# Dense tokens' rows kept in DRAM for most of the kernel, and gate blocks read back eight at a time instead of four

## The chip, the cores and the metric

The kernel runs on one core of a Trainium2 chip. The metric is the device time of one execution in microseconds (us), the median of several runs. The engines named below are PE (TensorE matmul), PEld (its weight loads), DVE (VectorE), ACT (ScalarE), POOL (GpSimd) and SP (SyncE, which here only issues transfers). The 16 DMA engines of the core serve three queues: q1 holds what SP issues, q10 what ACT issues, q0 the gathers that POOL issues.

## The reference, cut to what matters

The input has 512 tokens of 1024 channels. A first part (norm, a projection, pooling and convolution branches, gates, `w_out`) gives the residual row of each token. The second part is a retrieval of experts: each token picks 128 of 16384 experts (8 heads, 16 each) with softmax gates, and adds the weighted rows of `expert_v`.

```python
x = x + m @ w_out[l]                       # the residual rows
h2 = rmsnorm(x, g_ffn[l])
...
u = expert_u[idx]
act = jax.nn.gelu(jnp.einsum('thkd,td->thk', u, hb), approximate=False)
wts = (gates * act)
out = jnp.einsum('thk,thkd->td', wts, expert_v[idx])
...
return rmsnorm(x + out, g_final)
```

## The kernel before, in words

All arithmetic is float32, done on PE as three products of a high and a low part (fp32r). Tokens stand in four blocks of 128 (`NT`). Three blocks (`KD`, 384 tokens, the dense tokens) are treated densely: for each of 128 blocks of 128 experts the kernel makes the hidden values of all tokens with `expert_ut` (`u_mm`, 24 matmuls of 320 columns), multiplies them by a dense matrix of gates (`weigh`, L873), and adds the product with `expert_v` into six PSUM banks (`v_mm`, L894, 18 matmuls of 512 columns). For the fourth block, and for the `expert_u` half of 64 tokens of the third, POOL gathers single expert rows by index (L706) and DVE uses them (L718 the dot products, L723 the weighted sum).

The time falls into stages. Up to about 500 us the first part and the choice of keys run. Then the gates' matrix is built (to about 767 us): one-hot matmuls give it, ACT moves it into a stage, and ACT's queue writes stages of 32 tokens (`TG`) into a DRAM tile `Gd` of 11 x 128 x 128 x 32 numbers (the twelfth stays in SBUF). During these stages `u_mm` runs ahead for 76 blocks (`n_ahead`), whose hidden values go to DRAM (`Ad`).

The main loop (L945) then goes over the 128 expert blocks i in an order written out by hand. SP's queue gets, in this order, the load of `expert_v` for block i + 3 (`vr`, L751), the load of gates where one is due (`gt`, L773), and the load of hidden values for block i + 2 (`ab`, L786). While i + 1 is below 76 only `v_mm` runs on PE ("the v stage" below, about 797 to 1121 us); from then on `u_mm(i + 1)` and `v_mm(i)` ("the both stage", to about 1479 us), and SP's queue gets the `expert_ut` load (`ur`, L425) behind the gates' load. DVE's order in one turn of the v stage is: low part of `expert_v` for i + 2 (L871), gates times hidden values for i + 1 (L879, which needs `ab` and `gt`), low part of that product (L55, after ACT's high part, L54), then one or two gathered rows. Whatever DVE waits for holds all that stands behind it.

A gates' load brings `IG` = 4 expert blocks: `g_load(i + 2)` does so when i + 2 is a multiple of 4. In DRAM the numbers that lie together for one partition and one stage are `IG` x `TG`, 512 B. `g_rest` (L779) lets ACT copy the twelfth stage's part beside them. The tile has two buffers.

The residual rows `x1` (four blocks, 4 KB of each partition per block) stay in SBUF from the first load to the end: L385 adds the first part's output, L723 the gathered rows (fourth block), and after the last matmuls L903 adds the PSUM banks; then follow the last norm (L911) and the stores (L924).

Of the kernel before, what the change touches and what calls it, by code (L numbers as in the profile page):

```python
# [8 lines left out]
F32 = mybir.dt.float32  # L9
# [3 lines left out]
AF = mybir.ActivationFunctionType  # L13
ALU = mybir.AluOpType
AX = mybir.AxisListType

P = 128
D = 1024
T = 512
NT = T // P  # L20
DC = D // P
H = 8
TOPK = 16
NK = 128
# [5 lines left out]
KD = 3  # L30
# [6 lines left out]

R_BUILD, R_LATE = 0.93, 0.4

TG, IG = 32, 4  # L40


def f(ap):
# [4 lines left out]
def block_kernel(ctx: ExitStack, tc: tile.TileContext, io, out, dbg=None):  # L48
    nc = tc.nc
    dbg = dbg or {}  # L50
# [13 lines left out]
    def bank(i, dt=F32):  # L64
        return psum.tile([P, 512], dt, tag=f"b{i}", name=f"b{i}")
# [7 lines left out]
    keep = ctx.enter_context(tc.tile_pool(name="keep", bufs=1))  # L73
    work = ctx.enter_context(tc.tile_pool(name="work", bufs=2))

    wpool = tc.alloc_tile_pool(name="wpool", bufs=2, side="right", reuse_waits="tile")
    fpool = tc.alloc_tile_pool(name="fpool", bufs=1, reuse_waits="tile")

# [6 lines left out]
    yH, yL = yHL[:, 0], yHL[:, 1]  # L85


    x1 = keep.tile([P, NT, D], F32, name="x1")
    gb = fpool.tile([P, D], F32, tag="gb", name="gb")
    w0 = [wpool.tile([P, DC, 256], t, tag=n, name=n) for n, t in (("raw", F32), ("wh", F32R), ("wl", F32R))]  # L90

    def x_load(tb):
        nc.sync.dma_start(x1[:, tb], io["x"][tb * P:(tb + 1) * P])

    def w0_load(e):
        nc.sync.dma_start(w0[0][:, :, e * P:(e + 1) * P], io["w_in"][0, :, :, e * P:(e + 1) * P])
# [33 lines left out]
    def rms_sum(xs, junks):  # L130

        st = work.tile([P, 4, len(xs)], F32, tag="rms", name="st", bufs=3)
        for k, (x_tb, junk) in enumerate(zip(xs, junks)):
            nc.scalar.activation(junk, x_tb, AF.Square, accum_out=st[:, 0, k:k + 1])
        return st

    def rms_sqrt(st):

        nc.vector.tensor_scalar(st[:, 1], st[:, 0], 1.0 / D, EPS, op0=ALU.mult, op1=ALU.add)
        nc.scalar.activation(st[:, 2], st[:, 1], AF.Sqrt)  # L140

    def rms_inv(st):

        v, y, t = st[:, 1], st[:, 2], st[:, 3]
        nc.vector.reciprocal(y, y)
        nc.vector.tensor_tensor(t, y, y, ALU.mult)
        nc.vector.tensor_tensor(t, t, v, ALU.mult)
        nc.vector.tensor_scalar(t, t, -0.5, 1.5, op0=ALU.mult, op1=ALU.add)
        nc.vector.tensor_tensor(t, t, y, ALU.mult)
        return [t[:, k:k + 1] for k in range(st.shape[2])]  # L150

    def norm(tb, g, dst=None):

        xg = dst if dst is not None else wpool.tile([P, D], F32, tag="xg", name="xg")
        st = rms_sum([x1[:, tb]], [xg])
        rms_sqrt(st)
        nc.vector.scalar_tensor_tensor(xg, x1[:, tb], rms_inv(st)[0], g, op0=ALU.mult, op1=ALU.mult)
        return xg

    def norm_T(tb, xg, hH, hL, banks):  # L160
# [59 lines left out]
    xg, st = {}, {}  # L220

    def start(tb):
        xg[tb] = wpool.tile([P, D], F32, tag="xg", name="xg")
        st[tb] = rms_sum([x1[:, tb]], [xg[tb]])
        rms_sqrt(st[tb])

    def scale(tb, r=None):
        nc.vector.scalar_tensor_tensor(xg[tb], x1[:, tb], r if r is not None else rms_inv(st[tb])[0], gb, op0=ALU.mult, op1=ALU.mult)

    def w0_split(e):  # L230
        es = slice(e * P, (e + 1) * P)
# [74 lines left out]
    for hf in range(2):  # L306
        us = []
        wc = ws_q.pop(0)
        for e in range(2):
            zc = z_chunk(wc, e)  # L310
            cs = fpool.tile([P, T], F32, tag="u", name="cs", bufs=2)
# [6 lines left out]
        for e in range(2):  # L318
# [6 lines left out]
            g = hf * 2 + e  # L325
            y = fpool.tile([P, T], F32, tag="s", name="y", bufs=2)
# [6 lines left out]
        for e in range(2):  # L333
            zb = z_chunk(wb, e)
            p = fpool.tile([P, T], F32, tag="p", name="yb", bufs=2)
# [10 lines left out]
    for hf in range(4):  # L346
# [14 lines left out]
        for e in range(2):  # L361
# [4 lines left out]
            t = fpool.tile([P, T], F32, tag="s", name="t", bufs=2)  # L366
# [15 lines left out]

    def add_x(tb, hf, o):
        cs = slice(hf * 512, (hf + 1) * 512)
        nc.vector.tensor_tensor(x1[:, tb, cs], o, x1[:, tb, cs], ALU.add)  # L385

    os_ = [rbank() for _ in range(NT)]
    for q in range(2):
# [10 lines left out]
    for tb in range(NT):  # L399
        o = bank(2 + tb)  # L400
# [10 lines left out]
    upool = tc.alloc_tile_pool(name="upool", bufs=2, reuse_waits="tile")  # L411
# [4 lines left out]
    dram = ctx.enter_context(tc.tile_pool(name="dram", bufs=1, space=bass.MemoryType.DRAM))  # L416
# [32 lines left out]
    def u_act(i, o):  # L449
        a = upool.tile([P, TU], F32, tag="a", name="a", bufs=3)  # L450
        nc.scalar.activation(a, o[:, :TU], AF.Gelu)  # L451
        if i < n_ahead:
            nc.scalar.dma_start(Ad[i], a)
        else:
            hid[i] = a
# [31 lines left out]
    if TM:  # L487

        for q in range(2):
            nc.sync.dma_start(hm[q * TM:(q + 1) * TM], xgs[KD - 1][P - TM:])  # L490
    if "x1" in dbg:
        nc.sync.dma_start(dbg["x1"].rearrange("(n p) d -> p n d", p=P), x1)

    skT = qpool.tile([P, 2 * H, NK], F32, name="skT")
    nc.sync.dma_start(skT, io["sub_keys_t"])
# [182 lines left out]
    if "gate" in dbg:  # L678
        for nm, tl in (("gate", gate), ("key0", key[0]), ("key1", key[1])):
            nc.sync.dma_start(dbg[nm].rearrange("(n p) d -> p n d", p=P), tl.rearrange("p n h k -> p n (h k)"))  # L680
    wpool.release()
    qpool.release()


    gpool = tc.alloc_tile_pool(name="gpool", bufs=1, reuse_waits="tile")
    dots = upool.tile([P, NT - KD, P], F32, name="dots", bufs=1)
# [24 lines left out]
    def gather_use(upto):  # L711
        while n_done[0] < min(upto, len(plan)):
            n = n_done[0]
            kind, g, k = plan[n]
            r = rows.pop(n)
            if kind == "u":
                src, dst = (hm, mdots[:, TM + k:TM + k + 1]) if g is None else (hn[:, g], dots[:, g, k:k + 1])
                nc.vector.tensor_tensor_reduce(out=r, in0=r, in1=src, op0=ALU.mult, op1=ALU.add, scale=1.0,  # L718
                                               scalar=0.0, accum_out=dst)
                if g is not None and k % CH == CH - 1:  # L720
                    todo[n + 4] = todo[n + 8] = (g, slice(k - CH + 1, k + 1))
            else:
                nc.vector.scalar_tensor_tensor(x1[:, KD + g], r, dots[:, g, k:k + 1], x1[:, KD + g], op0=ALU.mult, op1=ALU.add)  # L723
            n_done[0] += 1
            if n in todo:

                g, cs = todo.pop(n)
                if n + 4 in todo:
                    nc.scalar.activation(dots[:, g, cs], dots[:, g, cs], AF.Gelu)
                else:  # L730
                    nc.vector.tensor_tensor(dots[:, g, cs], dots[:, g, cs], ggate[:, g, cs], ALU.mult)
# [37 lines left out]
    def g_load(i):  # L769
        if i < NK:  # L770
            if i % IG == 0:
                gt = bpool.tile([P, NG, IG, TG], F32, tag="gt", name="gt")
                nc.sync.dma_start(gt[:, :NG - 1].rearrange("p n i t -> p n (i t)"),  # L773
                                  Gd[:, :, i:i + IG, :].rearrange("n j i t -> j n (i t)"))
                gt_of[i] = gt
                for k in range(IG):
                    gts[i + k] = gt[:, :, k]

    def g_rest(i):  # L779
        if i < NK and i % IG == 0:  # L780
            nc.scalar.copy(gt_of[i][:, NG - 1], stages[0][:, i:i + IG])
# [35 lines left out]
    for n in range(0, TD // 4, 2):  # L817
# [14 lines left out]
        i = nu[0]  # L832
# [66 lines left out]
    gfin = keep.tile([P, D], F32, tag="hm", name="gfin")  # L899

    def add_acc(tb, hf):
        cs = slice(hf * 512, (hf + 1) * 512)
        nc.vector.tensor_tensor(x1[:, tb, cs], acc[tb][hf], x1[:, tb, cs], ALU.add)  # L903

    def fin_sum(tb, hf):

        if hf == 0:
            ys[tb] = (gpool.tile([P, D], F32, tag="gr", name="yo", bufs=GB), work.tile([P, 5, 1], F32, tag="rms", name="st", bufs=3))
        y, st = ys[tb]
        cs = slice(hf * 512, (hf + 1) * 512)  # L910
        nc.scalar.activation(y[:, cs], x1[:, tb, cs], AF.Square, accum_out=st[:, 4 * hf])  # L911
        if hf:
            nc.vector.tensor_tensor(st[:, 0], st[:, 0], st[:, 4], ALU.add)
            rms_sqrt(st)
# [4 lines left out]
    def fin_scale(tb, parts=1):  # L919
        y, _, r = ys.pop(tb)  # L920
        for q in range(parts):
            cs = slice(q * D // parts, (q + 1) * D // parts)
            nc.vector.scalar_tensor_tensor(y[:, cs], x1[:, tb, cs], r, gfin[:, cs], op0=ALU.mult, op1=ALU.mult)
            nc.sync.dma_start(out[tb * P:(tb + 1) * P, cs], y[:, cs])  # L924

    ys = {}
    acc = [[bank(2 + 2 * tb + hf) for hf in range(2)] for tb in range(KD)]
# [16 lines left out]
    units, spent, done0 = sum(cost[:NK - 7]), 0.0, n_done[0]  # L944
    for i in range(NK - 1):  # L945
        v_load(i + 3)
        g_load(i + 2)
        g_rest(i + 2)
        a_load(i + 2)
        both = i + 1 >= n_ahead  # L950
        spent += cost[i]
        want = done0 + int((len(plan) - done0) * min(1.0, spent / units))
        v_high(i + 2)
        v_low(i + 2)
        if both:
            u_load(i + 4)
            u_split(i + 3, nc.vector)
            o = u_mm(i + 1)
            u_act(i + 1, o)
        if i < NK - 3:  # L960
            v_mm(i)
        weigh(i + 1)
        for k in range(n_done[0], want):
            gather(k + 1, 2)
        if i == NK - 5:
            assert n_done[0] == len(plan)
            fin_sum(KD, 0)
            fin_sum(KD, 1)
            fin_inv(KD)
            fin_scale(KD)  # L970
# [74 lines left out]
```

## Time and profile before

| | |
|---|---|
| median of 3 runs | 1529.55 us (1529.26 to 1531.38) |
| the profiled execution | 1528.38 us, of which its span 1526.6 us |
| PE busy | 1475.6 us (97%) |
| PEld busy | 1292.6 us (85%) |
| DVE busy | 1229.3 us (81%) |
| ACT busy | 665.6 us (44%) |
| POOL busy | 730.7 us (48%) |
| DMA | 415.72 MB in 163357 packets, 272 GB/s on average |
| packets of SP's queue q1 | 102992, 210.99 MB, 38.6% of 16 engines' span |
| packets of POOL's queue q0 | 46144, 167.80 MB, 29.1% |

A share over the whole span is an average over stages with different limits, so the rows of single stages say more than this table. A matmul's record overlaps the next one's, so that busy time of PE is close to the stretch whenever it does not wait.

### The profile page before, as it was taken

How to read it: one execution, taken by the hardware profiler on the slowest of the kernel's cores; microseconds unless marked ns; L12 is line 12 of the kernel's file. 1: busy time of each engine (PE TensorE's matmuls, PEld its weight loads, DVE VectorE, ACT ScalarE, POOL GpSimd, SP SyncE). 2: the span in 40 equal slices, each digit the busy share in tenths (PEclk: the TensorE clock that was granted, in tenths of full speed). 3: DMA queues.
4: the chain of work that ended last, by engine and by line, in shares of the span. 5: the costliest groups of instructions: out<-in, count | busy, mean ns of one | idle time of the engine just before them, and what ended most of it. 6: DMA issues, size and time to landing. Idle time of an engine off the chain costs nothing.

```text
span 1526.6 us, 22154 instructions
## 1 busy us (share of the span) xinstructions
PE 1475.6 (97%) x7953; PEld 1292.6 (85%) x7953; DVE 1229.3 (81%) x2399; ACT 665.6 (44%) x1144; POOL 730.7 (48%) x432
## 2 busy tenths in 40 slices
PE   8999999999998999999999999999999999999997
PEld 6788888888888999998997878878789999999986
DVE  6842434649999999999988888888889999999985
ACT  4323223433334677776853433333343333333334
POOL 3432323237773454545244444444466676666620
PEclk9999999999999999999999999999999999999999
DMA  5222223432214899999999999999999999999971
GB/s 186 83 97 83 85 95 126 129 149 110 110 60 141 308 387 367 368 379 393 347 341 370 347 352 359 353 347 367 352 357 383 367 381 370 392 378 371 369 265 69
DMA packets 163357, 415.72 MB, mean 272 GB/s; under 512 B 13744, under 2 KB 80304, under 8 KB 156848
## 3 DMA queue, kind: packets, MB, share of 16 engines
q1 hardware_dynamic: 102992, 210.99, 38.6%
q0 software_dynamic: 46144, 167.80, 29.1%
q10 hardware_dynamic: 14112, 35.53, 6.1%
q8 instruction: 62, 1.02, 0.3%
q14 instruction: 47, 0.39, 0.1%
HBM read 376.05 MB, written 37.62 MB: 271 GB/s over the span
## 4 chain that ended last, share of the span: by engine, by line
DVE 41%; PE 40%; issue 10%; ACT 4%; DMA 3%; POOL 1%; DVEq 0%; ACTq 0%; SPq 0%; POOLq 0%
PE b L891 15%; PE b L59 8%; PE b L60 8%; PE b L58 8%; DVE gr L718 7%; DVE uL L434 5%; DVE x L723 5%; DVE vL L871 5%; ACT wH L54 2%; DVE oj L799 2%; DVE oi L799 2%; DVE gt L879 2%; DVE oj L810 1%; DVE eq L583 1%; PE b L852 1%
## 5 line engine op out<-in xcount | busy, mean ns | idle before, releaser
L60 PE MATMUL b<-h2H,uL 128*128 128x320 f32 x1024 | 320.9, 313 | 17.0 <-DVE uL L434 16.7
L58 PE MATMUL b<-h2H,uH 128*128 128x320 f32 x1024 | 322.8, 315 | 0.2 <-ACT h2H L54 0.2
L59 PE MATMUL b<-h2L,uH 128*128 128x320 f32 x1024 | 317.7, 310 | 1.0 <-DVE h2L L55 1.0
L706 POOL DMA_INDIRECT gr<-in_expert_u,gidx x128 | 204.3, 1596 | 219.2 <-DVE dots L718 126.2
L706 POOL DMA_INDIRECT gr<-in_expert_v,gidx x128 | 210.4, 1644 | 159.7 <-DVE x L723 95.5
L891 PE MATMUL b<-vH,wH 128*128 128x512 f32 x768 | 240.4, 394 | 9.4 <-ACT wH L54 9.4
L891 PE MATMUL b<-vL,wH 128*128 128x512 f32 x768 | 237.8, 390 | 0.0
L891 PE MATMUL b<-vH,wL 128*128 128x512 f32 x768 | 237.3, 390 | 0.0
L60 PEld LDWEIGHTS b<-h2H,uL 128*128 128x128 f32 x1024 | 193.7, 189 | 25.2 <-DVE uL L434 25.2
L59 PEld LDWEIGHTS b<-h2L,uH 128*128 128x128 f32 x1024 | 193.9, 189 | 3.2 <-DVE h2L L55 1.2
L58 PEld LDWEIGHTS b<-h2H,uH 128*128 128x128 f32 x1024 | 194.1, 190 | 2.5 <-ACT h2H L54 0.5
L54 ACT CAST wH<-gt 128x384 fp32r<-128x384 f32 x128 | 65.7, 513 | 286.1 <-DVE gt L879 267.0
L891 PEld LDWEIGHTS b<-vH,wH 128*128 128x128 f32 x768 | 141.4, 188 | 41.0 <-ACT wH L54 16.1
L867 ACT CAST vH<-vr 128x1024 fp32r<-128x1024 f32 x128 | 134.8, 1053 | 87.5 <-PE b L891 62.6
L891 PEld LDWEIGHTS b<-vL,wH 128*128 128x128 f32 x768 | 144.6, 188 | 30.9
L891 PEld LDWEIGHTS b<-vH,wL 128*128 128x128 f32 x768 | 144.5, 188 | 30.5
L723 DVE SCALAR_TENSOR_TENSOR x<-gr,dots,x 128x1024 f32<-128x1024 f32 x128 | 164.1, 1282 | 2.1
L871 DVE TENSOR_TENSOR vL<-vr,vH 128x1024 fp32r<-128x1024 f32 x128 | 156.4, 1222 | 9.7 <-ACT vH L867 7.5
L55 POOL TENSOR_TENSOR wl<-raw,wh 128x2048 fp32r<-128x2048 f32 (+1 forms) x21 | 79.3, 3777 | 155.9 <-ACT wh L54 155.9
L718 DVE CUSTOM_DVE_ANT_0 gr<-gr,hn 128x1024 f32<-128x1024 f32 x128 | 152.2, 1221 | 1.3 <-DMA gr<-in_expert_u,gidx 1.3
L430 ACT CAST uH<-ur 128x1024 fp32r<-128x1024 f32 x128 | 133.9, 1047 | 35.3 <-ACT a L451 18.4
L434 DVE TENSOR_TENSOR uL<-ur,uH 128x1024 fp32r<-128x1024 f32 x113 | 140.3, 1243 | 8.1 <-ACT uH L430 6.7
(216 smaller groups left out, 2511.2 us busy)
## 6 DMA issues: line engine op xcount, KB each, us to landing
ur<-in_expert_ut SPq DMA_DIRECT2D x128, 512.0 KB
vr<-in_expert_v SPq DMA_DIRECT2D x128, 512.0 KB
Gd<-stage ACTq DMA_DIRECT2D x22, 1024.0 KB
gt<-Gd SPq DMA_DIRECT2D x32, 704.0 KB
raw<-in_w_in SPq DMA_DIRECT2D x15, 1024.0 KB
Ad<-a ACTq DMA_DIRECT2D x76, 160.0 KB
ab<-Ad SPq DMA_DIRECT2D x76, 160.0 KB
raw<-in_w_q SPq DMA_DIRECT2D x8, 1024.0 KB
```

The lines of the kernel that those rows point to most:

```text
L54: nc.scalar.copy(Hd, src)
L58: nc.tensor.matmul(o, lh, rh, start=first, stop=False)
L59: nc.tensor.matmul(o, lh, rl, start=False, stop=False)
L60: nc.tensor.matmul(o, ll, rh, start=False, stop=last)
L430: nc.scalar.copy(us[i][0], raws[i])
L434: eng.tensor_tensor(us[i][1], raws.pop(i), f(us[i][0]), ALU.subtract)
L706: nc.gpsimd.indirect_dma_start(out=r, out_offset=None, in_=io["expert_u" if kind == "u" else "expert_v"], in_offset=bass.IndirectOffsetOnA ...
L718: nc.vector.tensor_tensor_reduce(out=r, in0=r, in1=src, op0=ALU.mult, op1=ALU.add, scale=1.0, scalar=0.0, accum_out=dst)
L723: nc.vector.scalar_tensor_tensor(x1[:, KD + g], r, dots[:, g, k:k + 1], x1[:, KD + g], op0=ALU.mult, op1=ALU.add)
L867: nc.scalar.copy(vs[i][0], vraw[i])
L871: nc.vector.tensor_tensor(vs[i][1], vraw.pop(i), f(vs[i][0]), ALU.subtract)
L891: nc.tensor.matmul(acc[tb][hf], lw[:, ts], rw[:, hf * 512:(hf + 1) * 512], start=i == 0 and rw is vH and lw is wH, stop=last and i == NK - 1)
```

## The change

The gates' load brings eight blocks, so the numbers that lie together are 1024 B, a load is 1408 KB instead of 704 KB, and there are 16 instead of 32. It is issued three blocks earlier (`g_load(i + 5)`). The tile's two buffers take 12 KB of each partition more. To make room, the residual rows of the three dense blocks live in a pool that is given up before the gates' matrix is built: once they are final they are written to a DRAM tile `Xd` (three stores of 512 KB on SP's queue, between the two small `hm` copies and the load of the sub keys, `skT`), and in the fourth-last turn of the main loop three loads of 512 KB bring them back into the buffers of `ur`.

```diff
-TG, IG = 32, 4
+TG, IG = 32, 8
...
+    xpool = tc.alloc_tile_pool(name="xpool", bufs=1, side="right", reuse_waits="tile")
     wpool = tc.alloc_tile_pool(name="wpool", bufs=2, side="right", reuse_waits="tile")
...
-    x1 = keep.tile([P, NT, D], F32, name="x1")
+    x1d = xpool.tile([P, KD, D], F32, name="x1d")
+    x1 = [x1d[:, tb] for tb in range(KD)] + [keep.tile([P, D], F32, name="x1g") for _ in range(NT - KD)]
...
+    Xd = dram.tile([KD, P, D], F32, name="Xd")
+    for tb in range(KD):
+        nc.sync.dma_start(Xd[tb], x1[tb])
 
     skT = qpool.tile([P, 2 * H, NK], F32, name="skT")
     nc.sync.dma_start(skT, io["sub_keys_t"])
...
     wpool.release()
+    xpool.release()
     qpool.release()
...
         v_load(i + 3)
-        g_load(i + 2)
-        g_rest(i + 2)
+        g_load(i + 5)
+        g_rest(i + 5)
         a_load(i + 2)
...
+        if i == NK - 4:
+
+            for tb in range(KD):
+                x1[tb] = upool.tile([P, DC, P], F32, tag=f"ur{tb}", name="xe", bufs=1).rearrange("p c t -> p (c t)")
+                nc.sync.dma_start(x1[tb], Xd[tb])
         if i < NK - 3:
             v_mm(i)
```

The rest of the diff writes `x1[tb]` for `x1[:, tb]`, and drops an output that is used only when looking for errors.

## Rows read from the trace of the kernel before

**Rows 1.** Busy time by stage: PE, PEld, DVE, ACT, POOL, PEclk, DMA share, GB/s.

```profile
797.00:1121.00 324.00, 316.14 (x1377) 257.43 (x1378) 270.55 (x369) 124.65 (x179) 152.28 (x92) 0.99 1.00 357
1121.00:1479.00 358.00, 357.81 (x1973) 323.95 (x1971) 328.12 (x401) 137.05 (x201) 226.95 (x142) 1.00 0.99 371
1479.00:1526.60 47.60, 38.93 (x204) 34.29 (x204) 27.01 (x57) 22.16 (x43) 0.00 (x0) 0.94 0.20 73
```

**Rows 2.** Waits in 797:1121: total us, times, longest.

```profile
DVE wL L55 <- ACT wH L54: 46.8, 76, 0.6
...
PE b L891 <- ACT wH L54: 8.9, 14, 2.2
...
DVE vL L871 <- ACT vH L867: 3.3, 9, 1.6
...
ACT vH L867 <- DMA vr<-in_expert_v: 1.0, 1, 1.0
...
DVE gt L879 <- DMA ab<-Ad: 0.5, 1, 0.5
```

**Rows 3.** DMA in 797:1121: queue, packets, MB, share; issues.

```profile
q1 hardware_dynamic: 48992, 66.90, 59.6%
q0 software_dynamic: 13203, 48.12, 39.5%
...
vr<-in_expert_v SPq DMA_DIRECT2D x76, 512.0 KB
gt<-Gd SPq DMA_DIRECT2D x19, 704.0 KB
ab<-Ad SPq DMA_DIRECT2D x73, 160.0 KB
```

**Rows 4.** DMA in 1121:1479, SP's queue.

```profile
q1 hardware_dynamic: 30460, 57.33, 43.9%
```

**Rows 5.** Timeline of SP, two stretches: start, duration, issue.

```profile
889.18 3.25 SPq L786 DMA_DIRECT2D ab<-Ad  x1
...
1074.27 1.35 SPq L786 DMA_DIRECT2D ab<-Ad  x1
```

**Rows 6.** Chain of waits in 880:905: start, duration, what.

```profile
889.18 10.21 DMA ab<-Ad
```

**Rows 7.** Timeline of DVE, the users of those two loads.

```profile
901.52 0.49 DVE L879 TENSOR_TENSOR gt<-ab,gt 128x320 f32<-128x320 f32 x1
...
1085.67 0.49 DVE L879 TENSOR_TENSOR gt<-ab,gt 128x320 f32<-128x320 f32 x1 [0.48 <-DMA ab<-Ad]
```

**Rows 8.** Tile gt: duration ns min/median/max, first and last start.

```profile
L54 ACT CAST wH<-gt x128: 511/513/516, 797.0 to 1507.1; 128x384 fp32r<-128x384 f32 x128
...
L773 SPq DMA_DIRECT2D gt<-Gd x32: 382/428/611, 766.9 to 1468.6; - x32
L781 ACT COPY gt<-stage x32: 292/294/299, 782.6 to 1479.2; 128x128 f32<-128x128 f32 x32
```

**Rows 9.** Timeline at the front, around the place of the new stores.

```profile
297.57 1.08 SPq L495 DMA_DIRECT2D skT<-in_sub_keys_t  x1
...
300.58 0.33 SPq L471 DMA_DIRECT2D raw<-in_w_q  x1
...
314.92 1.91 ACT L472 CAST wh<-raw 128x2048 fp32r<-128x2048 f32 x1
...
319.84 1.05 PE L538 MATMUL b<-skT,q 128*128 128x128 f32 x8
```

**Rows 10.** Timeline at the end, around the place of the new loads.

```profile
1494.34 1.88 SPq L751 DMA_DIRECT2D vr<-in_expert_v  x1
...
1494.93 1.22 DVE L434 TENSOR_TENSOR uL<-ur,uH 128x1024 fp32r<-128x1024 f32 x1
...
1499.64 1.05 ACT L867 CAST vH<-vr 128x1024 fp32r<-128x1024 f32 x1 [2.54 <-DMA vr<-in_expert_v]
...
1509.89 1.29 DVE L903 TENSOR_TENSOR x<-b,x 128x512 f32<-128x512 f32 x2 [1.71 <-PE b L891]
```

More of the change, by code (lines that the diff above doesn't have):

```diff
@@ L92, in x_load @@
     def x_load(tb):
-        nc.sync.dma_start(x1[:, tb], io["x"][tb * P:(tb + 1) * P])
+        nc.sync.dma_start(x1[tb], io["x"][tb * P:(tb + 1) * P])
     def w0_load(e):
@@ L154, in norm @@
         xg = dst if dst is not None else wpool.tile([P, D], F32, tag="xg", name="xg")
-        st = rms_sum([x1[:, tb]], [xg])
+        st = rms_sum([x1[tb]], [xg])
         rms_sqrt(st)
-        nc.vector.scalar_tensor_tensor(xg, x1[:, tb], rms_inv(st)[0], g, op0=ALU.mult, op1=ALU.mult)
+        nc.vector.scalar_tensor_tensor(xg, x1[tb], rms_inv(st)[0], g, op0=ALU.mult, op1=ALU.mult)
         return xg
@@ L223, in start @@
         xg[tb] = wpool.tile([P, D], F32, tag="xg", name="xg")
-        st[tb] = rms_sum([x1[:, tb]], [xg[tb]])
+        st[tb] = rms_sum([x1[tb]], [xg[tb]])
         rms_sqrt(st[tb])
     def scale(tb, r=None):
-        nc.vector.scalar_tensor_tensor(xg[tb], x1[:, tb], r if r is not None else rms_inv(st[tb])[0], gb, op0=ALU.mult, op1=ALU.mult)
+        nc.vector.scalar_tensor_tensor(xg[tb], x1[tb], r if r is not None else rms_inv(st[tb])[0], gb, op0=ALU.mult, op1=ALU.mult)
     def w0_split(e):
@@ L384, in add_x @@
         cs = slice(hf * 512, (hf + 1) * 512)
-        nc.vector.tensor_tensor(x1[:, tb, cs], o, x1[:, tb, cs], ALU.add)
+        nc.vector.tensor_tensor(x1[tb][:, cs], o, x1[tb][:, cs], ALU.add)
     os_ = [rbank() for _ in range(NT)]
@@ L490, in block_kernel @@
             nc.sync.dma_start(hm[q * TM:(q + 1) * TM], xgs[KD - 1][P - TM:])
-    if "x1" in dbg:
-        nc.sync.dma_start(dbg["x1"].rearrange("(n p) d -> p n d", p=P), x1)
+    Xd = dram.tile([KD, P, D], F32, name="Xd")
+    for tb in range(KD):
+        nc.sync.dma_start(Xd[tb], x1[tb])
     skT = qpool.tile([P, 2 * H, NK], F32, name="skT")
@@ L722, in gather_use @@
             else:
-                nc.vector.scalar_tensor_tensor(x1[:, KD + g], r, dots[:, g, k:k + 1], x1[:, KD + g], op0=ALU.mult, op1=ALU.add)
+                nc.vector.scalar_tensor_tensor(x1[KD + g], r, dots[:, g, k:k + 1], x1[KD + g], op0=ALU.mult, op1=ALU.add)
             n_done[0] += 1
@@ L902, in add_acc @@
         cs = slice(hf * 512, (hf + 1) * 512)
-        nc.vector.tensor_tensor(x1[:, tb, cs], acc[tb][hf], x1[:, tb, cs], ALU.add)
+        nc.vector.tensor_tensor(x1[tb][:, cs], acc[tb][hf], x1[tb][:, cs], ALU.add)
     def fin_sum(tb, hf):
@@ L910, in fin_sum @@
         cs = slice(hf * 512, (hf + 1) * 512)
-        nc.scalar.activation(y[:, cs], x1[:, tb, cs], AF.Square, accum_out=st[:, 4 * hf])
+        nc.scalar.activation(y[:, cs], x1[tb][:, cs], AF.Square, accum_out=st[:, 4 * hf])
         if hf:
@@ L922, in fin_scale @@
             cs = slice(q * D // parts, (q + 1) * D // parts)
-            nc.vector.scalar_tensor_tensor(y[:, cs], x1[:, tb, cs], r, gfin[:, cs], op0=ALU.mult, op1=ALU.mult)
+            nc.vector.scalar_tensor_tensor(y[:, cs], x1[tb][:, cs], r, gfin[:, cs], op0=ALU.mult, op1=ALU.mult)
             nc.sync.dma_start(out[tb * P:(tb + 1) * P, cs], y[:, cs])
```

## The prediction

> **What bounds the kernel now.** I read the busy times by stage first, since the change lives in the main loop. In the both stage PE is busy 357.81 of 358 us: it is the bound, alone [rows 1]. In the v stage three things are nearly full at once: PE is busy 316.14 of 324 us, DVE 270.55, and the DMA engines have a share of 1.00 [rows 1]. The next view, the waits of that stage, tells which of the three holds the others. DVE's idle time there is 53.45 us (324 less 270.55), and 46.8 of it is 76 waits of 0.6 us for ACT's high part, between two of its own steps [rows 2]; busy plus this wait is 317.35 us, so DVE is as full as PE. For transfers DVE waited 0.5 us in all, once, and ACT 1.0 us, once [rows 2]. So the DMA engines are full, but almost nobody is late because of them: loads are issued so far ahead that their latency is just covered. PE waits 8.9 us for DVE and ACT [rows 2]. The reader is to see that the v stage is held by PE and DVE together, with the DMA at the edge of becoming the third.
>
> **The change part by part.** Durations are those of the profiled execution: 1528.38 us, that is its span of 1526.6 and 1.8 outside it. It is 1.2 us under the median of 1529.55; I work out a difference and add it to the median.
>
> *What a gates' load costs the DMA engines.* The page has no time for one packet size, so I fit a fixed time per packet and a time per MB to the two rows of q1. In the v stage the packets took 59.6% of 324 x 16 us = 3090 us, for 48992 packets and 66.90 MB [rows 3]; in the both stage 43.9% of 358 x 16 = 2515 us, for 30460 and 57.33 MB [rows 4]. That gives 11.6 ns per packet and 37.7 us per MB (10^6 bytes). A packet of 512 B is then 30.9 ns, one of 1024 B 50.2 ns, one of 4096 B 166 ns, one of 1280 B (`ab`) 60 ns: estimates, all from these rows. A load of four blocks is 11 x 128 = 1408 packets of 512 B, on 16 engines 2.72 us; a load of eight is 1408 packets of 1024 B, 4.42 us. Eight blocks cost 5.44 us before and 4.42 after: 1.0 us less, 0.13 us a block. But one burst is 1.7 us longer.
>
> *Does the saving reach the time?* In the both stage it can't: PE never idles there. In the v stage a block takes 324 / 76 = 4.26 us. Without gates the DMA work of a block is 1.33 us (`vr`, 128 packets of 4096 B) plus 0.48 (`ab`) plus gathers, 39.5% of 324 / 76 = 1.68 [rows 3], in sum 3.49; gates add 0.68 before and 0.55 after. That is 4.17 against 4.04 of 4.26 us. A saving on engines for which DVE waited once counts for that one wait at most, 0.5 us; the ceiling, were the DMA really the bound, is PE's idle time in the stage, 324 less 316.14 = 7.9 us [rows 1]. I take 0.5, the nearer row.
>
> *The longer burst.* Right behind the gates' load in SP's queue stands `ab` for block i + 2, which DVE needs three turns later. It is the load that is late first. In one case it was issued at 889.18, landed 10.21 us later [rows 5, 6] and was used at 901.52, 2.1 us in hand [rows 7]; in another it was issued at 1074.27 and its user, free at 1085.19, waited 0.48 us until 1085.67: latency 11.4 at most, lead 10.9 [rows 5, 7]. So the lead is 10.9 to 12.3 us and the latency behind a burst 10.2 to 11.4. Before there are 18 bursts with an `ab` behind them (i = 2, 6, ..., 70), and the waits sum to 0.5 us. After there are nine (i = 3, 11, ..., 67), each 1.7 us longer. If each finds the queues as full as now, latency is 11.9 to 13.1 and DVE loses between nothing and 2.2 us each time. But the DMA has 4.26 - 3.49 = 0.77 us of spare time per block: a burst of 2.72 us needs 3.5 of its 4 blocks to be worked off, one of 4.42 us needs 5.7 of its 8. The next burst will find the queues emptier than today's do, so I count half of the 1.7 us. Then only the bursts at the short lead are late: I take one in three of nine, by 0.5 us (the wait of [rows 7]), 1.5 us in all. Bounds: minus 0.5 (no wait at all) and nine times 2.2 = 20 us. Behind the waiting multiply DVE holds the low parts and the gathered rows, and PE waits for them, so what DVE loses here PE loses. In the both stage no `ab` is loaded; behind the burst stands `ur`, needed two turns later, and PE has no idle time, so nothing is counted.
>
> *The gates themselves.* They come three blocks earlier than before, so that the load's own 1.7 us more cannot be late; the first is issued at 766.9 and first used by ACT's cast at 797.0 [rows 8]. Their buffer is free by then: block i + 5 takes the one last read at block i - 4. The ACT copy of the twelfth stage falls from 32 of 0.294 us to 16 of about 0.40 (0.294 for 128 numbers a partition, 0.513 for 384 [rows 8], so an estimate of 0.404 for 256): 2.9 us less on ACT, which is busy 124.65 of 324 us [rows 1], so 0. A longer copy ahead of the `expert_v` cast could hold DVE, whose waits there sum to 3.3 us [rows 2]: bounds minus 2 and plus 1, I take 0.
>
> *The stores into `Xd`.* They are three issues on SP's queue ahead of `skT`, and 384 packets of 4096 B, 4.0 us of DMA work by the fit. `skT` is issued at 297.57 and first used at 319.84, 22 us in hand; the next, `raw` of the second head's `w_q`, is issued at 300.58 and cast at 314.92, 14 us in hand, for `hm`, `skT`, `raw` and two `ur` (some 9 us by the fit) plus the 4.0 [rows 9]. Thin but enough: 0, with 2 us as the upper bound should the cast move.
>
> *The loads from `Xd`.* SP issues them behind the last `vr` (1494.34, 1.88 us); the second also needs the buffer of the last `ur`, read by DVE until 1496.15. Another 4.0 us of DMA work behind the last `vr`, which is there at 1499.64, ends near 1504; the first user runs at 1509.89 [rows 10]. They stand behind `vr`, so they don't delay it: 0, with 3 us as the upper bound. SP has nothing else to issue until the final stores.
>
> The sum: minus 0.5, plus 1.5, is plus 1.0 us; 1529.55 + 1.0 = 1530.5 us.
>
> **The rivals.**
>
> *The DMA is the bound.* For it: a share of 1.00 through the whole v stage [rows 1], SP held for 3.25 us in an issue behind a gates' load [rows 5], and PE's 7.9 idle us. Against it: 0.5 us of waits. Then 0.13 us a block times 76 is 9.9 us, of which PE's idle time allows 7.9: 1521.7 us. The Trainium skill speaks for this side: "DMA: Bandwidth & Descriptors", section "Rules for kernel authors", wants at least 1 MiB per DMA for full bandwidth, and the gates' load passes that size with this change. The trace shows full engines with 704 KB loads too, so it bears out the price per packet and not a gain in time.
>
> *The burst makes `ab` late (the slower side).* The place is L879 behind each of the nine loads, the price what the latency exceeds the lead by. It decides from the point where latency passes 10.9 us, which today's bursts already reach. If the emptier queue gives back little, about half of the bursts come at the long lead and lose 0.5, half at the short one and lose 1.5 us: nine times 1.0, less today's 0.5, is plus 8.5 us, 1538 us. The Trainium skill's same page, section "Queues, rings and completion order", says that an engine takes a queue's descriptors in ring order and alternates between queues packet by packet. By that rule `ab` waits for the whole load ahead of it, and gathers are served between: it would make the 1.7 us a lower bound of the shift and put this rival's time at 1538 or above. The trace agrees so far: `ab` behind a gates' load took 10.21 us for 160 KB [rows 6].
>
> *The change doesn't do what it says:* the 1024 B don't come as one packet, and the load is 2816 packets of 512 B. Then a burst is 5.44 us, nothing is saved, and the second rival's price grows to some 15 us: 1545 us. The numbers of one partition and stage do lie together on both sides, so I hold it for unlikely.
>
> **How the numbers follow.** Within 0.2% (3.06 us, about what a measurement can tell from no change) is 1526.5 to 1532.6. Forecast, no visible change: 0.62. DMA as the bound: 0.14, nearly all of it faster by over 0.2%. Late `ab`, packets that don't merge, or a late `Xd` load or store: 0.24, slower. The range reaches into both sides until about 0.1 is left out on each: 1524 to 1536.
>
> **What would show it.** Right: 16 gates' loads, each 1408 packets; q1's share in the v stage lower by two or three hundredths; PE still at about 316 us there; waits of L879 for `ab` of one to three us in all; no wait of L903 for a transfer. Wrong: PE's idle time in the v stage falling below 4 us (first rival), waits of L879 or of the `expert_v` cast for transfers above 5 us (second), the stages before 500 us or after 1479 us longer by more than 1 us (stores or loads of `Xd`).

## The result: 0.8% slower, and the profile after

The kernel after takes 1542.94 us (median of 6 runs, 1538.37 to 1545.06) against 1529.76 for the kernel before (6 runs, 1528.70 to 1531.38): ratio 1.0079, with a 95% interval of 1.0062 to 1.0096. The forecast was 1530.5, no visible change. The profiled execution is the shortest of the six, 1538.37 us with a span of 1536.6; what is placed below is its 10.0 us over the 1526.6 of before. The other executions of after lost up to 6.7 us more, and no profile of them exists.

The page of after: the work has not grown, the gates' loads are 16 of 1408 KB.

```profile
PE 1478.8 (96%) x7953; PEld 1292.6 (84%) x7953; DVE 1229.2 (80%) x2399; ACT 663.2 (43%) x1128; POOL 729.9 (48%) x432
...
gt<-Gd SPq DMA_DIRECT2D x16, 1408.0 KB
```

Where the time is lost is read from events that both kernels have: the issue of the first gates' load (L773 before, L778 after; the line numbers have moved by about five) and DVE's multiply of gates and hidden values (L879, L884). Times in us from the start, from the timelines of SP and DVE:

| | first gates' load | first multiply | block 76 (both stage begins) | first multiply to block 76 | span |
|---|---|---|---|---|---|
| before | 766.91 | 796.52 | 1121.77 | 325.25 | 1526.6 |
| after | 766.12 | 799.86 | 1131.65 | 331.79 | 1536.6 |
| difference | -0.8 | +3.3 | +9.9 | +6.5 | +10.0 |

So 4.1 us are lost between the first gates' load and the first multiply (33.74 us for 29.61; 3.3 of them show, since after came to that load 0.8 us sooner), 6.5 in the v stage, and nothing from there to the end. It is the distances that can be compared, not the times from the start: the issue of the first gates' load moves between 766.1 and 771.0 from one profiled execution to the next, whatever the kernel. From it to the first multiply it takes 29.6 to 30.0 us in the four profiles with a first load of four blocks, and 32.5 to 33.7 in the six where eight blocks come in one load.

The busy times by stage of after fit this (columns as in [rows 1]): PE is idle for 14.0 us of 797:1121 where it was idle for 7.9 [rows 1], in part because the stage begins later (PE waits 4.3 us for the first product, where it waited 1.6), and the DMA share has fallen to 0.96. Engines that are less full and a stage that is longer: somebody waits.

```profile
767.00:797.00 30.00, 28.74 (x204) 27.95 (x202) 19.39 (x29) 15.67 (x29) 10.13 (x7) 1.00 0.88 305
797.00:1121.00 324.00, 309.96 (x1325) 250.31 (x1326) 265.40 (x364) 119.49 (x163) 147.27 (x90) 0.98 0.96 348
1121.00:1479.00 358.00, 358.00 (x1970) 324.01 (x1969) 327.65 (x402) 137.49 (x196) 232.81 (x145) 1.00 0.99 375
```

The first of these stretches is the end of the build, which the forecast did not count as a stage. The same stretch of the kernel before:

```profile
767.00:797.00 30.00, 28.99 (x210) 28.73 (x208) 23.61 (x36) 16.58 (x32) 11.86 (x8) 1.00 0.94 328
```

DVE did 23.61 us of work in it before and 19.39 after. The next two fences are the waits of after in 797:1121 (answering to [rows 2]) and in 767:801.

```profile
DVE wL L55 <- ACT wH L54: 46.9, 74, 0.9
...
PE b L896 <- ACT wH L54: 14.4, 15, 4.3
...
ACT vH L872 <- DMA vr<-in_expert_v: 6.9, 7, 1.4
DVE gt L884 <- DMA ab<-Ad: 6.1, 4, 2.7
...
DVE vL L876 <- ACT vH L872: 1.9, 5, 0.8
```

```profile
DVE uL L436 <- ACT uH L432: 10.1, 2, 8.6
...
ACT uH L432 <- DMA ur<-in_expert_ut: 7.3, 2, 4.0
```

In the v stage DVE waits 6.1 us for `ab`, in four of nine bursts (0.36, 0.41, 2.60 and 2.73 us), against 0.5 once before [rows 2]: 5.6 us more, most of the stage's 6.5. The other 0.9 us are not accounted for by a wait shown here; ACT's waits for `vr` have grown too, from 1.0 to 6.9 us. In 767:801 ACT waits twice for `ur` and DVE then 8.6 us for ACT. Before, ACT waited there once, and DVE less:

```profile
DVE uL L434 <- ACT uH L430: 4.9, 2, 4.5
...
ACT uH L430 <- DMA ur<-in_expert_ut: 3.2, 1, 3.2
```

One burst of after, in the timelines of SP (first fence) and DVE (second), shows the mechanism; it answers to [rows 5, 7]. SP issues the gates' load, then `ab`, and is held 4.25 us in that issue. (This hold is not what grew: on the mean it is 2.3 us over the nine bursts, and was 2.1 over the eighteen of before.) `ab` lands when DVE has been idle for 2.73 us, 13.8 us after its issue began.

```profile
1085.57 0.43 SPq L778 DMA_DIRECT2D gt<-Gd  x1
1086.09 4.25 SPq L791 DMA_DIRECT2D ab<-Ad  x1
1090.44 1.02 SPq L756 DMA_DIRECT2D vr<-in_expert_v  x1
```

```profile
1099.95 0.49 DVE L884 TENSOR_TENSOR gt<-ab,gt 128x320 f32<-128x320 f32 x1 [2.73 <-DMA ab<-Ad]
```

The chain of waits of after (start, duration, what; pieces from several stretches) has these transfers in it. The `ur` stands behind the very first gates' load and two `ab`, the three `ab` stand right behind later gates' loads, and the `vr` is the second behind one; [rows 6] had 10.21.

```profile
772.11 14.09 DMA ur<-in_expert_ut
...
913.69 11.67 DMA ab<-Ad
...
955.61 10.48 DMA vr<-in_expert_v
...
982.53 13.55 DMA ab<-Ad
...
1086.09 13.83 DMA ab<-Ad
```

Packets and shares in the v stage (columns as in [rows 3]): SP's queue has 34440 packets where it had 48992, and 56.5% where it had 59.6%.

```profile
q1 hardware_dynamic: 34440, 65.02, 56.5%
q0 software_dynamic: 13015, 47.41, 38.8%
```

### The profile page after: what moved, and what is told of

Same layout as the page of the kernel before. It is cut to its first block, busy times and chain, and to the rows that moved or that the text cites. A ratio compares the mean times of both kernels' runs of the same rounds, so it can differ in the third digit from the quotient of the medians.

```text
span 1536.6 us, 22152 instructions
## 1 busy us (share of the span) xinstructions
PE 1478.8 (96%) x7953; PEld 1292.6 (84%) x7953; DVE 1229.2 (80%) x2399; ACT 663.2 (43%) x1128; POOL 729.9 (48%) x432
## 4 chain that ended last, share of the span: by engine, by line
DVE 41%; PE 38%; issue 10%; DMA 6%; ACT 4%; POOL 1%; DVEq 0%; SPq 0%; ACTq 0%; POOLq 0%
PE b L896 13%; PE b L59 8%; PE b L60 8%; PE b L58 8%; DVE gr L723 7%; DVE x1g L728 5%; DVE vL L876 5%; DVE uL L436 5%; DMA ab<-Ad 3%; ACT wH L54 2%; DVE oj L804 2%; DVE gt L884 2%; DVE oi L804 2%; DMA ur<-in_expert_ut 2%; PE b L857 1%
## 5 line engine op out<-in xcount | busy, mean ns | idle before, releaser
L728 DVE SCALAR_TENSOR_TENSOR x1g<-gr,dots,x1g 128x1024 f32<-128x1024 f32 x128 | 164.0, 1281 | 2.1
```

The costliest lines, as they stand in the source:

```text
L728: nc.vector.scalar_tensor_tensor(x1[KD + g], r, dots[:, g, k:k + 1], x1[KD + g], op0=ALU.mult, op1=ALU.add)
```

## The experiments

Each time is a median, each ratio stands against the kernel before on the same chip, with its 95% interval. Edits are made to the kernel after, except where "the kernel before" is named. Latencies (issue to landing) are worked out from the trace's semaphore updates: the last update that a load makes; they are means, except where a median is named. A burst is what SP issues for the gates at one place, and a load's lead is the time from its issue until its user is ready for it. Theory A: a longer burst in SP's queue makes whatever stands behind it late (`ur` behind the first, `ab` behind the later ones). Rivals: the parked rows cost the time; the larger packet does; the DMA engines are the bound.

**Parking alone.** Gates by four again, the rows still in `Xd`.

```diff
-TG, IG = 32, 8
+TG, IG = 32, 4
...
-        g_load(i + 5)
-        g_rest(i + 5)
+        g_load(i + 2)
+        g_rest(i + 2)
```

> The residual rows are parked in DRAM as in the change, but gates come back four blocks at a time, two blocks ahead, as before. Theory (loads that stand behind the longer gates' load come late): parking costs nothing, 1530 us, within 1.5 us of the kernel before; waits of the multiply by the gates for ab at most 1 us. Rival (the parking costs: its stores at the front, its loads at the end, or the other places in SBUF): 1535 us or more, with most of the changed kernel's 13 us.

Measured: 1530.69 us, 1.0003 [0.9993, 1.0013]. `Xd` costs nothing that can be measured; the loss comes with the gates' loads.

**First load in halves.** The very first gates' load alone is split; its second half is issued after the first of the `u_mm` steps that close the build.

```diff
+    def g_part(i, n0, n1):
+        if i in gt_of:
+            nc.sync.dma_start(gt_of[i][:, n0:n1].rearrange("p n i t -> p n (i t)"),
+                              Gd[n0:n1, :, i:i + IG, :].rearrange("n j i t -> j n (i t)"))
...
-            g_load(0)
+            g_load(0, 6)
             a_load(0)
...
         u_tick(1, nc.vector)
+        if k == 0:
+            g_part(0, 6, NG - 1)
```

> The changed kernel, but only the first gates' load is in two parts: stages 0 to 5 at the old place, 6 to 10 behind the first expert_ut load after the build. Theory (late behind the burst): the expert_ut load for block 74 is no longer 4 us late, 3 to 4 us are won, 1539 us; the v stage is as in the changed kernel. Rival (that wait is covered by others): no gain, 1543 us.

Measured: 1536.11 us, 1.0043 [1.0029, 1.0057], so 6.8 us less than after, where 3 to 4 were expected. Only 2.3 of them lie between the two profiled executions (1536.07 and 1538.37, the shortest of after). From the first gates' load to the first multiply it takes 31.09 us, where after took 33.74 and before 29.61. The waits of this kernel in 767:1131: ACT waits for `ur` 3.2 us once, as before the change, and DVE still waits for `ab`.

```profile
DVE gt L888 <- DMA ab<-Ad: 5.7, 5, 1.9
ACT uH L432 <- DMA ur<-in_expert_ut: 3.2, 1, 3.2
```

**Main loop's loads in halves.** The first load stays whole; each later one is issued as stages 0 to 5, and 6 to 10 two turns later (`g_part` as above).

```diff
-        g_load(i + 5)
+        g_load(i + 5, 6)
+        if (i + 3) % IG == 0:
+            g_part(i + 3, 6, NG - 1)
         g_rest(i + 5)
```

> The changed kernel, but in the main loop each load of eight blocks goes out in two parts, stages 0 to 5 at the old place and 6 to 10 two turns later, with the same packets of 1024 B. The first load stays whole. Theory (late behind the burst): the waits for ab in the v stage go from 6 us to under 1 us, the 4 us at the first load stay: 1533 to 1535 us. Rival (the packets of 1024 B hold gathers and other loads up, whatever the burst's length): no change, 1541 to 1544 us. Rival (parking): no change.

Measured: 1531.74 us, 1.0013 [1.0004, 1.0022]: 11.2 us less than after, more than expected. No wait for `ab` is left in its trace; PE's busy time in the v stage is back at 314 us (columns as in [rows 1]).

```profile
797.00:1121.00 324.00, 314.00 (x1367) 255.96 (x1368) 272.38 (x372) 123.59 (x169) 154.18 (x92) 0.99 0.98 357
```

The two gains, 6.8 and 11.2, are more than the loss of 13.2; they don't add. The multiplies show where: with the main halves the first one comes at 800.12 (32.48 us from the first gates' load, 2.9 more than before), but block 76 at 1123.40, so the v stage is 2.0 us shorter than before and wins back part of what the first load lost. With the first load alone in halves they come at 797.74 and 1128.75, and the v stage keeps its loss (331.01 us). Why a late start is won back was not tested.

**Both in halves.** The two edits together.

> The changed kernel with every gates' load, the first one too, in two parts of 1024 B packets, two turns apart. Theory: both losses are gone, 1529 to 1531 us, the kernel before. Should the smaller DMA work of 1024 B packets be worth time (the rival that the DMA is the bound): 1526 us or less.

Measured: 1528.92 us, 0.9994 [0.9985, 1.0003]. The whole loss is gone, with parked rows, 1024 B packets and eight blocks at a time all kept. Nor is there a gain from the larger packets. Behind a half `ab` takes 9.19 us, as it did behind 704 KB (9.22).

```profile
797.00:1121.00 324.00, 315.09 (x1373) 256.79 (x1373) 270.76 (x370) 123.60 (x169) 152.18 (x91) 0.99 0.98 356
```

**Quarters.** As both halves, but the later loads in 3 + 3 + 3 + 2 stages over four turns.

```diff
+        g_load(i + 5, 3)
+        for p in range(1, 4):
+            if (i + 5 - p) % IG == 0:
+                g_part(i + 5 - p, 3 * p, min(3 * p + 3, NG - 1))
```

> The changed kernel with each gates' load of the main loop in four parts (3, 3, 3 and 2 stages) in four successive turns, the first load in two. Bursts of 1.2 us by the fit, 1024 B packets. Theory: no load is late for a burst, and what is left of the v stage is DVE and PE: 1528 to 1530 us, as with halves. If shorter bursts are worth more than halves: 1526 us or less.

Measured: 1528.88 us, 0.9992 [0.9983, 1.0001], the same as halves. Once nothing is late behind the burst, a shorter one brings nothing. This and the halves are the best versions found, and neither can be told from the kernel before.

**Two loads back to back.** Eight blocks as two loads of four, one right behind the other: packets of 512 B as before, but a burst of 2816 of them.

```diff
-                nc.sync.dma_start(gt[:, :NG - 1].rearrange("p n i t -> p n (i t)"),
-                                  Gd[:, :, i:i + IG, :].rearrange("n j i t -> j n (i t)"))
+                for k in (0, 4):
+                    nc.sync.dma_start(gt[:, :NG - 1, k:k + 4].rearrange("p n i t -> p n (i t)"),
+                                      Gd[:, :, i + k:i + k + 4, :].rearrange("n j i t -> j n (i t)"))
```

> The changed kernel, but each load of eight blocks is issued as two loads of four blocks, one right behind the other: packets of 512 B as before, bursts as long as two old ones (5.4 us by the fit, against 4.4). Theory (the burst's length): as slow as the changed kernel or slower, 1543 to 1550 us. Rival (the packet size): back to 1530 us.

Measured: 1552.63 us, 1.0145 [1.0129, 1.0160], the slowest of all full kernels and above the 1543 to 1550 expected. Packets of the old size don't bring the time back, so their size is not the cause. Counted from the burst's first issue, `ab` lands after 13.5 us, where it is 12.5 in after and 9.8 before. But SP also stands 4.2 to 5.8 us in each `ab` issue behind a burst (0.6 to 4.3 in after), so that `vr` is issued later too; how the 9.7 us over after divide between the longer burst and this hold was not tested. Its waits in 767:1131 (the last is before ACT's cast of `ur`; the gates' load is what the profile names):

```profile
DVE gt L885 <- DMA ab<-Ad: 14.2, 5, 3.7
...
ACT vH L873 <- DMA vr<-in_expert_v: 6.1, 8, 1.6
ACT uH L432 <- DMA gt<-Gd: 5.4, 1, 5.4
```

**`ab` ahead of the gates.** The order in SP's queue changed, so that `ab` is issued before the burst.

```diff
         v_load(i + 3)
+        a_load(i + 2)
         g_load(i + 5)
         g_rest(i + 5)
-        a_load(i + 2)
```

> The changed kernel with the ab load issued ahead of the gates' load of the same turn instead of behind it; the first load is untouched. Theory (late behind the burst): this ab is no longer late, the next one has a turn more for the burst to pass, waits for ab fall from 6 to under 2 us, 1534 to 1537 us. If the burst hurts by keeping all 16 engines busy rather than by standing ahead in SP's queue: little is won, 1541 us or more.

Measured: 1539.30 us, 1.0070 [1.0054, 1.0086]; 1534 to 1537 was expected, a miss. The waits for `ab` are gone, and `vr`, now the first load behind the burst, is late instead (waits in 767:1131):

```profile
ACT vH L872 <- DMA vr<-in_expert_v: 13.3, 9, 2.6
...
DVE vL L876 <- ACT vH L872: 5.7, 7, 1.6
```

**`ab` a turn earlier.** `ab` three blocks ahead, in four buffers.

```diff
-            abs_[i] = bpool.tile([P, TU], F32, tag="ab", name="ab", bufs=3)
+            abs_[i] = bpool.tile([P, TU], F32, tag="ab", name="ab", bufs=4)
...
             a_load(1)
+            a_load(2)
...
-        a_load(i + 2)
+        a_load(i + 3)
```

> The changed kernel with ab loaded three blocks ahead instead of two (four buffers instead of three), so that its lead is a turn, some 4 us, longer than the 11 to 12 us of now. Theory (the latency behind the burst passes the lead): latencies of 12 to 14 us stay, the waits for ab go to 0; 1534 to 1537 us, the rest being the first load. If something else holds DVE and ab only shows it: no gain, 1541 us or more.

Measured: 1539.94 us, 1.0057 [1.0044, 1.0071]; 1534 to 1537 was expected, again a miss. No wait for `ab`, and again `vr` takes its place (waits in 767:1131):

```profile
ACT vH L873 <- DMA vr<-in_expert_v: 16.6, 10, 3.3
...
DVE vL L877 <- ACT vH L873: 8.3, 8, 2.2
```

These two say that `ab` was only the first in line. Its lead can be made long enough, and the burst then delays the next load.

**`ab` on ACT's queue.** In the main loop `ab` is issued by ACT and no longer stands behind the burst.

```diff
-        a_load(i + 2)
+        a_load(i + 2, nc.scalar)
```

> The changed kernel with the main loop's ab loads issued by ACT, so that they stand in queue q10 and not behind the gates' load in q1. If ring order makes ab late (descriptors of one queue are taken in order, queues alternate packet by packet): latency of ab behind a burst falls from 12 to some 5 to 7 us, its waits go to 0, 1534 to 1537 us, unless ACT's own issue time (0.3 us a turn) costs. If the engines being busy makes it late, whatever the queue: latency stays at 10 us or more, 1541 us or more.

Measured: 1545.73 us, 1.0111 [1.0093, 1.0129]; 1534 to 1537 was expected, a miss. An `ab` that ACT issues within half a us of a gates' load now lands 7.05 us after its issue, where it took 11.89 behind the gates. The Trainium skill, "DMA: Bandwidth & Descriptors", section "Queues, rings and completion order", has an engine start the descriptors of one queue in order and take turns between queues; this trace agrees (7.05 against 11.89 us). But the gates' load itself now takes 13.5 us where it took 11.5, and ACT issues `ab` behind its own casts, later than SP did: its lead at the nine bursts' blocks is 8.0 us on the mean, where it was 11.7 in after. So `ab` is late at seven of the nine bursts and six times elsewhere, and `vr` is late as well (waits in 767:1131):

```profile
ACT vH L872 <- DMA vr<-in_expert_v: 12.4, 6, 3.5
DVE gt L884 <- DMA ab<-Ad: 10.1, 13, 1.7
...
DVE vL L876 <- ACT vH L872: 6.6, 6, 2.8
```

**Light gates.** The kernel before; from the third gates' load on, ten of its eleven stages are left out (and the tile keeps older gates in their place).

```diff
-                gt = bpool.tile([P, NG, IG, TG], F32, tag="gt", name="gt")
+                if i < 2 * IG:
+                    gt, n1 = bpool.tile([P, NG, IG, TG], F32, tag="gt", name="gt"), NG - 1
+                else:
+                    gt, n1 = gt_of[i - 2 * IG], 1
+                nc.sync.dma_start(gt[:, :n1].rearrange("p n i t -> p n (i t)"),
+                                  Gd[:n1, :, i:i + IG, :].rearrange("n j i t -> j n (i t)"))
```

> The kernel before, leaving out ten of the eleven stages of every gates' load from the third on (old numbers are used in their place). The DMA work of gates falls by nine tenths, 0.6 us a block in the v stage. If the DMA bounded the v stage (the rival of the prediction): PE's idle time there goes, 1522 us or less. If DVE and PE bound it and the DMA is full but covered: 1528 to 1530 us.

Measured: 1528.14 us, 0.9989 [0.9980, 0.9998]. The DMA share of the v stage falls from 1.00 [rows 1] to 0.91, PE stays at 315.58 us, and the time falls by 1.5 us. A stage with a DMA share of 1.00 was not bound by its DMA.

```profile
797.00:1121.00 324.00, 315.58 (x1377) 257.30 (x1376) 271.24 (x371) 124.35 (x178) 153.97 (x92) 0.99 0.91 321
```

**No gathered rows in the v stage**, in after and in before: the gathers move out of the stage, to where they cost time (1663.13 and 1668.69 us, one run each), and only the stage itself is read.

```diff
-    cost = [3.4 if i + 1 >= n_ahead else 1.25 for i in range(NK - 1)]
+    cost = [3.4 if i + 1 >= n_ahead else 0.0 for i in range(NK - 1)]
```

> The changed kernel with no gathered rows in the v stage (they all come in the both stage, which grows; only the v stage is looked at). If gathers served between its packets stretch a burst, the latency of ab behind a gates' load falls from 11.9 us to 8 or 9, some 4.4 us above that of an ab with nothing ahead of it. If the gates' load itself is slower than the fit's 4.4 us: it stays at 11 us or more.

> The same with the kernel before: latency of ab behind a gates' load falls from 9.2 us to 6 or 7, some 2.7 us above that of an ab with nothing ahead of it, 1.7 us under that of the changed kernel without rows.

Measured, the DMA issues in 797:1121 (last column: median us to landing), first with loads of eight blocks, then with loads of four:

```profile
gt<-Gd SPq DMA_DIRECT2D x10, 1408.0 KB, 8.8
ab<-Ad SPq DMA_DIRECT2D x73, 160.0 KB, 3.8
```

```profile
gt<-Gd SPq DMA_DIRECT2D x19, 704.0 KB, 5.8
ab<-Ad SPq DMA_DIRECT2D x73, 160.0 KB, 4.0
```

Right behind a burst `ab` takes 8.45 us with eight blocks and 5.96 with four, 2.49 apart, where 1.7 was expected; with the gathers it is 11.89 and 9.22, 2.67 apart. The gathers lengthen both and hardly touch the difference. An `ab` just ahead of a burst takes 3.6 us with loads of four (median; 3.7 with eight). Over these 3.6 us the burst adds 4.85 and 2.36 us (2.1 without the stage's first burst, the one slow case with 10.03 us): for twice the bytes a little over twice the jump, though the number of packets is the same.

**All profiles side by side.** From the first multiply to block 76 it takes 323.3 to 325.3 us in the six profiles in which the main loop's loads bring four blocks, come in parts or are light (before, parking alone, main halves, both halves, quarters, light gates), and 328.3 to 342.7 in the six in which each burst brings eight blocks (after, first load in halves, two loads back to back, and the three that move `ab`). From block 76 to the end eleven of the twelve take 404.2 to 405.6 us, and two loads back to back 407.6.

## Why the prediction was wrong

- *What bounds the stage.* Right. PE and DVE hold the v stage and the DMA is covered: light gates took nine hundredths of DMA share away for 0.0011 of the time. In the both stage PE is busy 358.00 of 358 us, and nothing is lost there.
- *The saving doesn't reach the time.* Right: both halves keep the saving and the ratio is 0.9994. The first rival falls with it. The Trainium skill, "DMA: Bandwidth & Descriptors", section "Rules for kernel authors", wants at least 1 MiB per DMA for full bandwidth; here 1408 KB in one load cost 0.8%, and its halves, under 1 MiB each, cost nothing.
- ***The longer burst*: the step that failed.** It was "The next burst will find the queues emptier than today's do, so I count half of the 1.7 us", and then one in three of nine late by 0.5 us, 1.5 in all; four were late, by 6.1 us in all. Three things in it were off. The shift of `ab` was 2.67 us, not 0.85: the packets in the v stage took 29.0 ns (512 B) and 52.7 ns (1024 B) on the mean in the trace, where the fit gave 30.9 and 50.2, so that a burst went from 2.55 to 4.64 us, 2.1 more and not 1.7; where the rest of the 2.67 comes from is not shown. The emptier queue gave back nothing that the shift shows: with the gathers, where the last `ab` ahead of a burst took 6.71 us before and 6.10 after, it is 2.67, and without them, where that `ab` takes 4.0 us with either load, 2.49. And the loss is set by the worst bursts, not by a typical one: two of nine made 5.3 of the 6.1 us. The second rival had the place and the mechanism of the v stage's loss and came near its size (8.5 us, where 6.5 were lost in the profiled execution); its 1538 lacks what the first load cost, and it was given too small a chance.
- ***The gates themselves*: also failed.** "They come three blocks earlier than before, so that the load's own 1.7 us more cannot be late" asks only who uses the gates. Behind the first load stands `ur`, for which ACT already waited 3.2 us before the change (waits of 767:801 above); the prediction has no row of that stretch and counts nothing there. It cost 4.2 us of DVE's time (a wait of 8.65 for one of 4.46) and 4.1 on the way from the first gates' load to the first multiply, and splitting this one load took 6.8 us off the median.
- *`g_rest`'s copy* takes 0.401 us where 0.404 was estimated, and ACT's idle time behind these copies fell from 8.0 to 3.1 us in 797:1121.
- *Stores into and loads from `Xd`:* 0, right (parking alone 1.0003). `raw`'s cast runs at 313.92, a microsecond earlier than before [rows 9], and L908 waits 1.71 us for PE, as before [rows 10], and for no transfer.
- *The change does what it says:* 14552 packets fewer in 797:1121, share 3.1 points lower, as the signs of the prediction wanted. The trace has 22528 packets of 1024 B, which is 16 loads of 1408, so the third rival falls.
- *The sign to look for* was there too: waits of L884 and of the `expert_v` cast for transfers are 6.1 and 6.9 us, above the 5 named for the second rival, and PE's "about 316 us" became 309.96.

Open stays why a late start is won back with the main halves, and why the other executions of after are up to 6.7 us longer than the profiled one; with both halves the spread is 2.4 us (1527.78 to 1530.20), which fits bursts that are late by more or less, but no profile shows it.

## What to carry to other kernels

Before you make a load larger, list what stands behind it in its queue, at every place where it is issued, the first included, and compare latency with lead for each of these: twice the bytes in one load delayed the `ab` behind it by 2.7 us, and made `ur` and `vr` late as well. If the leads are thin, issue the larger load in pieces some turns apart; moving one victim ahead, or to another queue, only chose the next. A DMA share of 1.00 says nothing of a bound until somebody is seen to wait.

## What the runs showed of the hardware that was not expected

- With the same number of packets, a load of twice the bytes delayed the load behind it by about twice as much (4.85 against 2.36 us over an undisturbed 3.6, without gathers); from one to the other the step was 2.49 us without gathers and 2.67 with them.
- How long SP stood in the `ab` issue behind a gates' load went with the packets ahead, not with their bytes: in the v stage 2.1 us on the mean behind 1408 packets of 512 B, 2.3 behind 1408 of 1024 B, 5.1 behind 2816 of 512 B, and 0.5 behind halves of 768 or 640 of 1024 B.
- A load moved off the busy queue landed sooner (7.05 us for 11.89), but the gates' load that it left took 2 us longer, 13.5 for 11.5.
